# Transposes of the first unit in all PSUM buffers, evacuations split by buffer, and the second unit's transposes moved to the third and fourth store tile

## Chip, cores, metric

One core of a Trainium2 chip. The metric is the device time of one execution in microseconds.

## The reference

```python
def setup_inputs():
    batch, heads, seq, dim = 8, 8, 512, 64
    ...   # q and k, float32

def reference(q, k):
    scale = 1.0 / np.sqrt(q.shape[-1])
    return (np.einsum('bhqd,bhkd->bhqk', q, k) * scale).astype(np.float32)
```

q and k together are 16.78 MB, the scores 67.11 MB. Four bytes out for each byte in, and little arithmetic between.

## The kernel before

The batch is cut into four units. A unit's k and q are loaded into one "big" buffer (4.19 MB), cast to bf16 by GpSimd, transposed by TensorE into PSUM in eight groups of eight, and copied out of PSUM (VectorE and ScalarE take the groups in turn, four copies a group). A unit gives four store tiles of 4.19 MB. A store tile also takes a "big" buffer, is filled by eight evacuations of PSUM, and leaves in one DMA. Three "big" buffers serve loads and stores in turn.

```python
    big_pool = ctx.enter_context(tc.tile_pool(name="big", bufs=3))
    tpsum_pool = ...(name="tpsum", bufs=2, space=PSUM)      # transposes
    psum_pool = ...(name="psum", bufs=3, space=PSUM)        # scores

    def evacuate(dst, src):
        if n_evac % 6 in (0, 2, 3):
            pinned(nc.scalar.mul(out=dst, in_=src, mul=scale))
        else:
            pinned(nc.vector.tensor_scalar(out=dst, in0=src, scalar1=scale, ...))
        n_evac += 1

    # transpose(v, kb, qb) is a generator: 8 groups of 5 steps
    # (one step of 8 TensorE transposes, four steps of one PSUM copy)

    def scores(v, t):
        o = big_pool.tile([P, 2, RO, S], f32, name="big")
        for x in range(2):
            for i in range(0, RO, 2):
                ps = psum_pool.tile([P, 2, S], f32, name="ps")
                ...                                         # two matmuls
                evacuate(o[:, x, i:i + 2, :], ps)
                yield
        nc.sync.dma_start(out=out_r[v, t], in_=o...)

    cast = [load_and_cast(v) for v in range(UNITS)]
    for _ in transpose(0, *cast[0]):
        pass
    for v in range(UNITS):
        ahead = transpose(v + 1, *cast[v + 1]) if v + 1 < UNITS else iter(())
        for t in range(TILES):
            for n, _ in enumerate(scores(v, t)):
                take(ahead, 1 + (t > 0 if v == 0 else n % 4 == 3))
```

The order of work on each engine is the order of the program. So the last line is a schedule: it says beside which store tile the next unit's transposes are done.

## Time and profile before

| | before |
|---|---|
| median of the first 3 runs | 202.94 us (202.80 to 202.94) |
| span of the trace | 201.3 us |
| busiest compute engine | VectorE, 63% of the span |
| data queue, share of the 16 DMA engines' time | 98.1% |
| bytes at the steady 430 GB/s | 83.89 MB / 0.43 = 195.1 us |

In all lines of the profiler PE is TensorE's matmuls and PEld its weight loads, DVE is VectorE, ACT ScalarE, POOL GpSimd and SP the sync engine, which issues the DMAs; L82 is line 82 of the kernel.

### The profile page before, as it was taken

How to read it: one execution, taken by the hardware profiler on the slowest of the kernel's cores; microseconds unless marked ns; L12 is line 12 of the kernel's file. 1: busy time of each engine (PE TensorE's matmuls, PEld its weight loads, DVE VectorE, ACT ScalarE, POOL GpSimd, SP SyncE). 2: the span in 40 equal slices, each digit the busy share in tenths (PEclk: the TensorE clock that was granted, in tenths of full speed). 3: DMA queues.
4: the chain of work that ended last, by engine and by line, in shares of the span. 5: the costliest groups of instructions: out<-in, count | busy, mean ns of one | idle time of the engine just before them, and what ended most of it. 6: DMA issues, size and time to landing. Idle time of an engine off the chain costs nothing.

```text
span 201.3 us, 1456 instructions
## 1 busy us (share of the span) xinstructions
PE 99.2 (49%) x503; PEld 48.3 (24%) x512; DVE 126.4 (63%) x130; ACT 100.7 (50%) x129; POOL 30.6 (15%) x22
## 2 busy tenths in 40 slices
PE   0033366753976729463729554856535666710000
PEld 0033353321522414231315221432212222200000
DVE  6726659995989929796749796569635264530000
ACT  2016667786674856583837663856515341510000
POOL 1277777556000000000000000000000000000000
PEclk9999999998599996999975998888995857555555
DMA  6999999999999999999999999999999999999993
GB/s 205 430 443 430 420 433 440 420 407 427 433 436 425 422 443 427 430 423 440 430 423 433 433 430 427 440 430 423 433 436 430 410 446 433 420 423 433 433 427 163
DMA packets 5510, 83.97 MB, mean 417 GB/s; under 512 B 384, under 2 KB 384, under 8 KB 384
## 3 DMA queue, kind: packets, MB, share of 16 engines
q1 hardware_dynamic: 5504, 83.89, 98.1%
q8 instruction: 4, 0.07, 0.1%
q14 instruction: 2, 0.02, 0.0%
HBM read 16.78 MB, written 67.11 MB: 417 GB/s over the span
## 4 chain that ended last, share of the span: by engine, by line
DMA 63%; DVE 16%; PE 3%; POOL 3%; ACT 1%; POOLq 1%; issue 1%; SPq 0%; DVEq 0%; ACTq 0%
DMA out_dram<-big 43%; DMA big<-in_q_dram 20%; DVE big L66 12%; PE ps L132 3%; DVE qz L95 3%; POOL xb L82 3%; DVE kT L95 1%; ACT big L64 1%; POOLq L186 1%; SPq L78 0%; DVEq L66 0%; SPq L137 0%; ACTq L64 0%; POOLq L82 0%
## 5 line engine op out<-in xcount | busy, mean ns | idle before, releaser
L132 PE MATMUL ps<-kT,qz 128*128 128x512 bf16 x247 | 81.1, 450 | 55.1 <-ACT big L64 39.2
L66 DVE TENSOR_SCALAR big<-ps 128x1024 f32<-128x1024 f32 x64 | 76.3, 1222 | 39.9 <-DMA out_dram<-big 29.1
L64 ACT ACTIVATE big<-ps 128x1024 f32<-128x1024 f32 x64 | 63.7, 1023 | 57.0 <-DMA out_dram<-big 30.8
L132 PEld LDWEIGHTS <-qz 128*128 128x128 bf16 x256 | 27.5, 111 | 96.0 <-issue 83.2
L82 POOL CAST xb<-big 128x2048 bf16<-128x2048 f32 x16 | 29.9, 1896 | 17.6 <-DMA big<-in_k_dram 11.9
L95 DVE COPY kT<-tp 64x512 bf16<-64x512 bf16 x32 | 22.0, 687 | 6.3 <-PE tp L107 5.7
L95 ACT COPY kT<-tp 64x512 bf16<-64x512 bf16 x32 | 18.5, 578 | 14.7 <-PE tp L107 14.4
L95 DVE COPY qz<-tp 64x512 bf16<-64x512 bf16 x32 | 22.0, 687 | 3.1 <-PE tp L116 2.7
L95 ACT COPY qz<-tp 64x512 bf16<-64x512 bf16 x32 | 18.5, 578 | 3.9 <-PE tp L116 3.6
L107 PE MATMUL tp<-identity,xb 128*128 128x128 bf16 x128 | 12.0, 254 | 16.5 <-POOL xb L82 12.5
L116 PE MATMUL tp<-identity,xb 128*128 128x128 bf16 x128 | 12.8, 265 | 6.0 <-DVE kT L95 3.5
L107 PEld LDWEIGHTS <-xb 128*128 128x128 bf16 x128 | 10.5, 116 | 20.8 <-POOL xb L82 12.8
L116 PEld LDWEIGHTS <-xb 128*128 128x128 bf16 x128 | 11.3, 122 | 10.9 <-issue 8.9
L147 DVE MEMSET qz<- 128x4096 uint32 x2 | 6.9, 3472 | 2.5 <-PEq L175 1.7
L95 ACT ACT_TABLE_LOAD x1 | 1.3, 1283 | 0.7 <-PEq L175 0.7
masks.py:199 POOL TENSOR_SCALAR_AFFINE_SELECT identity<-identity 128x128 bf16<-128x128 bf16 x1 | 0.3, 294 | 0.1
masks.py:197 POOL MEMSET identity<- 128x128 bf16 x1 | 0.2, 205 | 0.3 <-POOLq L175 0.3
L175 POOL MEMSET const-float32-0.0<- 128x1 f32 x1 | 0.1, 99 | 0.2 <-issue 0.2
L175 POOL MEMSET const-bfloat16-1.0<- 128x1 bf16 x1 | 0.1, 102 | 0.0
L175 POOL MEMSET const-uint8-127<- 128x1 uint8 x1 | 0.1, 102 | 0.0
L175 POOL MEMSET const-float32-1.0<- 128x1 f32 x1 | 0.1, 99 | 0.0
## 6 DMA issues: line engine op xcount, KB each, us to landing
out_dram<-big SPq DMA_DIRECT2D x16, 4096.0 KB, 21.4
big<-in_k_dram SPq DMA_DIRECT2D x4, 2048.0 KB, 19.2
big<-in_q_dram SPq DMA_DIRECT2D x4, 2048.0 KB, 24.2
```

What stands on the lines that cost most here:

```text
L64: pinned(nc.scalar.mul(out=dst, in_=src, mul=scale))
L66: pinned(nc.vector.tensor_scalar(out=dst, in0=src, scalar1=scale, scalar2=None, op0=mybir.AluOpType.mult))
L82: pinned(nc.gpsimd.tensor_copy(out=xb[:, :, s, :], in_=xf[:, x, s].rearrange("p (j d) -> p j d", j=J)))
L95: pinned(copy(out=dst(s, h), in_=src[:, h]))
L107: pinned(nc.tensor.transpose(out=tp[:, j, :], identity=identity, in_=kb[:, j0 + j].rearrange("p s d -> p (s d)")))
L116: pinned(nc.tensor.transpose(out=tp[:, i, jj, :], identity=identity, in_=qb[:, RO * jj + i0 + i].rearrange("p s d -> p (s d)")))
L132: pinned(nc.tensor.matmul(out=ps[:, w, :], lhsT=qz[:, i + w, n, :], rhs=kT[:, n].rearrange("d m s j -> d (m s j)"), start=True, stop=True))
L147: nc.vector.memset(qz, 0.0)
L175: nc = _bacc.Bacc("TRN2", target_bir_lowering=False, num_devices=1)
L186: with _tile.TileContext(nc) as tc:
```

## The change

It means to get the first store out sooner. (1) Half of the first k cast moves from GpSimd to VectorE. (2) The first unit's transposes may also use the scores' PSUM buffers, which are idle then, so that groups need not wait for each other. (3) Evacuations go ScalarE, ScalarE, VectorE, so that with three buffers each buffer has one engine. (4) The second unit's transposes are not begun beside the first two store tiles, but done beside the third (three steps after each evacuation) and the fourth (two).

```diff
-        if n_evac % 6 in (0, 2, 3):
+        if n_evac % 3 < 2:
             pinned(nc.scalar.mul(out=dst, in_=src, mul=scale))
...
-                pinned(nc.gpsimd.tensor_copy(out=xb[:, :, s, :], ...
+                copy = nc.vector.tensor_copy if v == x == s == 0 else nc.gpsimd.tensor_copy
+                pinned(copy(out=xb[:, :, s, :], in_=...))
...
+        def transposed(rows):
+            if v == 0 and n_tp % 4 > 1:
+                tp = psum_pool.tile([P, W, P], bf16, name="ps")
+            else:
+                tp = tpsum_pool.tile([P, W, P], bf16, name="tp")
...
-                take(ahead, 1 + (t > 0 if v == 0 else n % 4 == 3))
+                take(ahead, (0, 0, 3, 2)[t] if v == 0 else 1 + (n % 4 == 3))
```

(The order in which the two PSUM pools are made also changes; the two transpose loops are folded into one helper.)

More of the change, by code (lines that the diff above doesn't have):

```diff
@@ L35 @@
     JJ = J // RO
-    IW = 8 // JJ
     TILES = N // 2
@@ L50 @@
     t_pool = ctx.enter_context(tc.tile_pool(name="t", bufs=2))
+    psum_pool = ctx.enter_context(tc.tile_pool(name="psum", bufs=3, space=bass.MemoryType.PSUM))
     tpsum_pool = ctx.enter_context(tc.tile_pool(name="tpsum", bufs=2, space=bass.MemoryType.PSUM))
-    psum_pool = ctx.enter_context(tc.tile_pool(name="psum", bufs=3, space=bass.MemoryType.PSUM))
     pinned = tc.keep_in_program_order
@@ L81, in load_and_cast @@
             for s in range(2):
-                pinned(nc.gpsimd.tensor_copy(out=xb[:, :, s, :],
-                                             in_=xf[:, x, s].rearrange("p (j d) -> p j d", j=J)))
+                copy = nc.vector.tensor_copy if v == x == s == 0 else nc.gpsimd.tensor_copy
+                pinned(copy(out=xb[:, :, s, :], in_=xf[:, x, s].rearrange("p (j d) -> p j d", j=J)))
             both.append(xb)
@@ L103, in transpose @@
         ts[v] = (kT, qz)
-        for j0 in range(0, J, 8):
-            tp = tpsum_pool.tile([P, 8, P], bf16, name="tp")
-            for j in range(8):
-                pinned(nc.tensor.transpose(out=tp[:, j, :], identity=identity,
-                                           in_=kb[:, j0 + j].rearrange("p s d -> p (s d)")))
+        W = 8
+        def transposed(rows):
[3 more added lines that the diff above has]
+                tp = tpsum_pool.tile([P, W, P], bf16, name="tp")
+            for w, row in enumerate(rows):
+                pinned(nc.tensor.transpose(out=tp[:, w, :], identity=identity,
+                                           in_=row.rearrange("p s d -> p (s d)")))
+            return tp
+        for j0 in range(0, J, W):
+            tp = transposed([kb[:, j0 + j] for j in range(W)])
             yield
             yield from rearrange(tp, "d j (n h m) -> d h n m j",
-                                 lambda s, h: kT[half(h), :, :, s, j0:j0 + 8])
+                                 lambda s, h: kT[half(h), :, :, s, j0:j0 + W])
+        IW = W // JJ
         for i0 in range(0, RO, IW):
-            tp = tpsum_pool.tile([P, IW, JJ, P], bf16, name="tp")
-            for i in range(IW):
-                for jj in range(JJ):
-                    pinned(nc.tensor.transpose(out=tp[:, i, jj, :], identity=identity,
-                                               in_=qb[:, RO * jj + i0 + i].rearrange("p s d -> p (s d)")))
+            tp = transposed([qb[:, RO * jj + i0 + i] for i in range(IW) for jj in range(JJ)])
             yield
-            yield from rearrange(tp, "d i jj (n h m) -> d h i n m jj",
+            yield from rearrange(tp.rearrange("p (i jj) c -> p i jj c", jj=JJ),
+                                 "d i jj (n h m) -> d h i n m jj",
                                  lambda s, h: qz[half(h), i0:i0 + IW, :, h * U:(h + 1) * U]
```

## The prediction

> **What bounds the kernel now.** I read the rates first, then the stores, then the chain, then the groups. The page first:
>
> ```profile
> span 201.3 us, 1456 instructions
> ...
> DMA  6999999999999999999999999999999999999993
> ...
> q1 hardware_dynamic: 5504, 83.89, 98.1%
> ...
> HBM read 16.78 MB, written 67.11 MB: 417 GB/s over the span
> ```
>
> No compute engine is above 63% (VectorE), but the 16 DMA engines are at nine tenths or more in 38 of 40 slices, and the data queue alone fills 98.1% of their time. So the first question is whether there is any stretch in which the DMA waits for the compute engines. I asked for busy time by stage, cut where loads (to 33 us), loads just before the first store (33 to 38), loads beside stores (38 to 45) and stores alone (from 45) begin, then for the last 18 us before the tail:
>
> ```profile
> 5.00:33.00 28.00, 11.18 (x89) 8.72 (x91) 17.04 (x21) 12.25 (x19) 18.67 (x10) 1.00 1.01 431
> 33.00:38.00 5.00, 2.69 (x22) 1.41 (x20) 4.89 (x6) 3.12 (x5) 3.74 (x2) 1.00 1.01 426
> 38.00:45.00 7.00, 4.51 (x31) 2.18 (x29) 6.84 (x9) 6.30 (x9) 3.74 (x2) 1.00 1.01 417
> 45.00:190.00 145.00, 80.85 (x369) 35.95 (x374) 94.31 (x97) 77.73 (x97) 3.74 (x2) 0.81 1.01 430
> ...
> 178.00:196.00 18.00, 0.00 (x0) 0.00 (x0) 0.15 (x1) 0.00 (x0) 0.00 (x0) 0.50 1.01 431
> ```
>
> The last two columns are DMA share and GB/s. The share is 1.01 in every stage: the DMA is never short of work. It moves 430 GB/s beside busy engines and 431 when all compute has ended. The one soft spot is 417 while loads and stores overlap, still fully busy. The arithmetic closes: 83.89 MB at 430 GB/s is 195.1 us; counting back from the 1.43 MB of data that I find moved by 6 us (332 GB/s from 2 to 6 us, 98 before, less 0.09 MB of instruction fetch), the stream starts in effect at 2.7 us, so it ends at 197.8. The trace has it thinning out from 197 to 198.5, then completion, and 201.3 is the end. The start (first load issue 0.74 us) and the tail (about 3 us) are touched by no line of the diff.
>
> The DMA can only be delayed if a store comes too late. Each store tile is 4.19 MB, 9.75 us at that rate. With the queue served about in order, all that is queued before store i runs out at 2.7 + (16.78 + 4.19 i)/0.43: 41.7, 51.5, 61.2, 71.0, 80.7 us for i = 0 to 4. When were the first four issued? From the timeline of the sync engine:
>
> ```profile
> 38.23 0.40 SPq L137 DMA_DIRECT2D out_dram<-big  x1
> 46.05 0.39 SPq L137 DMA_DIRECT2D out_dram<-big  x1
> 58.31 0.37 SPq L137 DMA_DIRECT2D out_dram<-big  x1
> 63.61 0.37 SPq L137 DMA_DIRECT2D out_dram<-big  x1
> ```
>
> Slack before the queue runs dry: 3.5, 5.4, 2.9 and 7.4 us; the fifth, at 71.19, has 9.5. It stays 8 to 10 us later (the last is issued at 178.21, against 188). The chain of waits shows why the third store is as late as 58.31:
>
> ```profile
> 17.70 27.22 DMA big<-in_q_dram
> ...
> 45.07 1.90 POOL xb L82
> 46.96 1.85 POOLq L186
> 48.81 0.02 issue
> 48.84 1.23 DVE big L66
> ```
>
> The three "big" buffers are shared by loads and store tiles. Tile 2 takes the buffer of the fourth unit's load, whose q lands at 44.92 and is cast by GpSimd until 48.81. By the same rotation tile 0 needs unit 1's casts done (27.1 us) and tile 1 unit 2's (36.9).
>
> The durations used below:
>
> ```profile
> L66 DVE TENSOR_SCALAR big<-ps 128x1024 f32<-128x1024 f32 x64 | 76.3, 1222 | 39.9 <-DMA out_dram<-big 29.1
> L64 ACT ACTIVATE big<-ps 128x1024 f32<-128x1024 f32 x64 | 63.7, 1023 | 57.0 <-DMA out_dram<-big 30.8
> L95 DVE COPY kT<-tp 64x512 bf16<-64x512 bf16 x32 | 22.0, 687 | 6.3 <-PE tp L107 5.7
> L95 ACT COPY kT<-tp 64x512 bf16<-64x512 bf16 x32 | 18.5, 578 | 14.7 <-PE tp L107 14.4
> ```
>
> The longest wait of both evacuating engines is for a store to land (29.1 and 30.8 us): they already wait for the DMA, not the DMA for them.
>
> [...]
>
> **The change, part by part.**
>
> First cast on VectorE. It starts when the memsets end (9.40 us; k has landed at 8.7) and beside it GpSimd does the other half (8.7 to 10.6). [...]PE began its transposes at 12.49. [...]The q casts wait for their load (13.57) and end at 17.3 either way, so unit 3's load is still issued at 17.33.
>
> First transposes in four PSUM buffers. Before, groups went in pairs: PE at 12.49, 16.83, 20.82, 25.12, and the last copy ended at 27.03 + 2.35 = 29.4. Now the k groups run without a stop: PE 11.8 to 15.6 (16 transposes took 1.89), VectorE from 12.8 does two groups of 4 x 0.69 (to 18.3), ScalarE two groups of 4 x 0.58. The q groups, ready at 17.3, follow in free buffers: VectorE 18.4 to 24.0. So unit 0 is ready at about 24 instead of 29.4: 5.4 us less. But tile 0's buffer is free only at 27.1, so 3.1 us of this is lost to a wait that takes its place.
>
> Tiles 0 and 1 without transposes. Evacuations now go ScalarE, ScalarE, VectorE: tile 0 has six on ScalarE, 6 x 1.02 = 6.1 us. Store 0 is issued at about 27.1 + 6.2 = 33.4 (before 38.2); store 1, from 36.9 with five (5.1 us), at about 42.4 (before 46.1).
>
> Tile 2 with 24 of the 40 transpose steps. It starts at 48.8 as before. VectorE has three evacuations (3.7) and eleven copies, of which two run before 48.8: 3.7 + 9 x 0.69 = 9.9 us; plus half a microsecond for PE where two transposes' buffers are handed over: 59.2, against 58.3. Its deadline is 61.2: slack 2.0. Tile 3 with 16 steps: ScalarE has six evacuations and six copies to its last one, 6.1 + 3.5 = 9.6, so 59 + 10 = 69; deadline 71.0, slack 2.0. Tile 4, at 5.4 ScalarE evacuations and four copies plus waits, some 8.2 us: 77.5 against 80.7. From there a tile takes about 8 us in a period of 9.75, and slack grows again.
>
> Whole-kernel load: ScalarE 86 x 1.02 + 64 x 0.58 = 125 us, VectorE 42 x 1.22 + 44 + 7 + 1 = 103: the two swap places, and neither is near 201.
>
> Sum on the path that sets the end: start 0, stream 0, tail 0. One small term: the stage of mixed loads and stores starts 4.8 us earlier, at 417 instead of 430 GB/s, which costs 4.8 x 0.03 = 0.15 us. 202.94 + 0.1 = 203.0.
>
> **The rivals.** (a) The earlier first store moves the end: the intent, and 4.8 us would make it 198. For it: the last store hangs from the first through three buffers. Against it: the DMA is full at 38 us and after; an earlier store only makes the queue longer. (b) A hole opens at 61 or 71 us. Transposes that ran in the idle time before 48.8 are now packed behind it, and slack falls to 2 us at two stores. Each microsecond beyond it is one on the end. If both tiles take 2 us more than I sum, tile 3 is 2 us late: 205. The 16 DMA engines also need not run dry together, so a small loss may begin before the deadline. This is my main risk. (c) ScalarE becomes the bound at two thirds of the evacuations: 5.45 + 2.3 = 7.8 us a tile, under 9.75; no. (d) Longer mixing of loads and stores delays unit 3's q (already 2 to 3 us behind the 4.9 us rhythm of the earlier loads): then tile 2 slips and (b) gets its time.
>
> **Range and chances.** Only (b) and (d) have size, and both lengthen; (a) is limited to what is not stream now, under 0.5 us. So the range is narrow below and wider above: 202.4 to 204.5. Faster by 2% would need 199: 1%. Slower by 2% needs a hole of 4 us: 4%.
>
> **What would show it.** The DMA row at nine in the same 38 slices and about 430 GB/s from 45 to 190 us; store 0 issued near 33 us and store 1 near 42, with the last store still landing at the same time; unit 0's last copy near 24 us, then a wait of some 3 us for GpSimd's cast; stores 2 and 3 near 59 and 69; ScalarE near 125 us and VectorE near 103. A slice under nine near 61 or 71 us would mean rival (b). An end earlier by more than a microsecond would prove me wrong about the stream.

What before's trace has is 430 GB/s beside work and 431 without, and 1896 ns for GpSimd's cast of 128x2048. The sum came to 202.94 + 0.1 = 203.0. From the 12.49 of before's trace the same steps end 0.7 us later, at 24.7, still ahead of the 27.1 at which tile 0's buffer is free, so the stores' times stand. The half microsecond for PE in tile 2 and the waits in tile 4's 8.2 us were estimates. That the 16 DMA engines need not run dry together is seen at the end of before's trace: their mean busy share is 0.69, 0.31 and 0.08 in the microseconds from 197, 198 and 199.

## The result

The changed kernel is correct and takes 203.31 us (median of 4; 203.16 to 203.41) against 202.94 of the kernel before (median of 4; 202.80 to 203.24). The ratio is 1.0015, with a 95% interval of 0.9998 to 1.0033: the same. Ratios here and below are the mean time of one kernel's fast runs over that of the other's of the same rounds, so not quite the ratio of the medians.

The page of the kernel after, its span, its DMA row, the data queue and the rate:

```profile
span 201.3 us, 1459 instructions
...
DMA  6999999999999999999999999999999999999993
...
q1 hardware_dynamic: 5504, 83.89, 98.1%
...
HBM read 16.78 MB, written 67.11 MB: 417 GB/s over the span
```

The DMA row is the same digit for digit. The stages of the kernel after, cut at the same times as in the prediction (start:end and length; busy us of PE, PEld, DVE, ACT and POOL, with instruction counts; granted clock, DMA share, GB/s):

```profile
5.00:33.00 28.00, 13.92 (x83) 8.96 (x85) 18.16 (x21) 14.83 (x22) 18.59 (x9) 0.88 1.01 431
33.00:38.00 5.00, 0.71 (x3) 0.19 (x2) 1.22 (x1) 1.48 (x3) 3.73 (x3) 0.96 1.00 423
38.00:45.00 7.00, 5.91 (x31) 2.78 (x32) 3.82 (x5) 3.65 (x4) 4.52 (x3) 0.78 1.01 410
45.00:190.00 145.00, 79.62 (x387) 36.58 (x393) 76.07 (x83) 99.72 (x123) 2.94 (x2) 0.82 1.01 430
```

The compute columns have changed in every row. The DMA share has not, and the last row's rate is 430 as before. Only the stage of loads beside stores is slower: 423 and 410 GB/s where it was 426 and 417.

The stores did move. The sync engine's timeline of the kernel after, first five stores (start, duration, engine, line, operation):

```profile
33.28 0.40 SPq L143 DMA_DIRECT2D out_dram<-big  x1
42.92 0.39 SPq L143 DMA_DIRECT2D out_dram<-big  x1
58.44 0.37 SPq L143 DMA_DIRECT2D out_dram<-big  x1
67.16 0.37 SPq L143 DMA_DIRECT2D out_dram<-big  x1
74.55 0.37 SPq L143 DMA_DIRECT2D out_dram<-big  x1
```

The first goes out 5.0 us sooner, the second 3.1 us sooner, the third at the same time, the fourth and fifth 3.6 and 3.4 us later. In the chain of waits of the kernel after, the third tile still hangs from the last load and its cast:

```profile
17.54 26.52 DMA big<-in_q_dram
...
44.21 1.89 POOL xb L82
46.10 1.85 POOLq L192
47.95 0.02 issue
47.98 1.22 DVE big L65
```

And the groups of the kernel after, the two evacuations and the two casts (busy us, mean ns of one, idle time before and what ended most of it):

```profile
L63 ACT ACTIVATE big<-ps 128x1024 f32<-128x1024 f32 x86 | 84.4, 1023 | 43.2 <-DMA out_dram<-big 20.0
L65 DVE TENSOR_SCALAR big<-ps 128x1024 f32<-128x1024 f32 x42 | 51.4, 1225 | 66.2 <-DMA out_dram<-big 34.3
L82 POOL CAST xb<-big 128x2048 bf16<-128x2048 f32 x15 | 29.8, 2012 | 16.9 <-DMA big<-in_k_dram 10.8
...
L82 DVE CAST xb<-big 128x2048 bf16<-128x2048 f32 x1 | 1.2, 1165 | 0.0
```

The page gives ScalarE 121.0 us busy (before 100.7) and VectorE 102.6 (126.4): they swapped places, and both evacuating groups still wait above all for stores to land.

### The profile page after: what moved, and what is told of

Its sections match the earlier page's. It is cut to its first block, busy times and chain, and to the rows that moved or that the text cites. A ratio compares the mean times of both kernels' runs of the same rounds, so it can differ in the third digit from the quotient of the medians.

```text
span 201.3 us, 1459 instructions
## 1 busy us (share of the span) xinstructions
PE 100.2 (50%) x503; PEld 48.5 (24%) x512; DVE 102.6 (51%) x109; ACT 121.0 (60%) x151; POOL 30.5 (15%) x21
## 3 DMA queue, kind: packets, MB, share of 16 engines
q1 hardware_dynamic: 5504, 83.89, 98.1%
## 4 chain that ended last, share of the span: by engine, by line
DMA 61%; ACT 9%; PE 7%; DVE 5%; POOL 3%; issue 1%; POOLq 1%; ACTq 1%; SPq 0%
DMA out_dram<-big 41%; DMA big<-in_q_dram 19%; ACT big L63 8%; PE ps L138 5%; POOL xb L82 3%; PE tp L111 2%; DVE big L65 2%; DVE kT L94 2%; DVE qz L94 1%; POOLq L192 1%; ACT kT L94 1%; ACT qz L94 1%; ACTq L192 0%; SPq L77 0%; ACTq L63 0%
## 5 line engine op out<-in xcount | busy, mean ns | idle before, releaser
L63 ACT ACTIVATE big<-ps 128x1024 f32<-128x1024 f32 x86 | 84.4, 1023 | 43.2 <-DMA out_dram<-big 20.0
L65 DVE TENSOR_SCALAR big<-ps 128x1024 f32<-128x1024 f32 x42 | 51.4, 1225 | 66.2 <-DMA out_dram<-big 34.3
L111 PE MATMUL tp<-identity,xb 128*128 128x128 bf16 x224 | 21.0, 252 | 18.1 <-POOL xb L82 13.6
L94 ACT COPY kT<-tp 64x512 bf16<-64x512 bf16 x28 | 16.2, 578 | 12.5 <-PE tp L111 12.2
L94 DVE COPY kT<-tp 64x512 bf16<-64x512 bf16 x28 | 19.2, 687 | 4.7 <-PE tp L111 4.4
L94 DVE COPY qz<-tp 64x512 bf16<-64x512 bf16 x28 | 19.2, 687 | 0.4
L94 ACT COPY qz<-tp 64x512 bf16<-64x512 bf16 x28 | 16.2, 578 | 0.5 <-PE tp L111 0.2
L111 PE MATMUL ps<-identity,xb 128*128 128x128 bf16 x32 | 3.8, 312 | 0.0
L94 DVE COPY kT<-ps 64x512 bf16<-64x512 bf16 x4 | 2.8, 689 | 0.1
L94 DVE COPY qz<-ps 64x512 bf16<-64x512 bf16 x4 | 2.8, 689 | 0.1
```

The source lines that it names most:

```text
L94: pinned(copy(out=dst(s, h), in_=src[:, h]))
L111: pinned(nc.tensor.transpose(out=tp[:, w, :], identity=identity, in_=row.rearrange("p s d -> p (s d)")))
```

## The experiments

All runs give the reference's result except where it is said. Times are medians. "Store 1" to "store 4" are the issue times of the first four stores in the trace. By the prediction's sum, all that is queued before them runs out at 41.7, 51.5, 61.2 and 71.0 us; I call these the dry times.

| run | store 1 | store 2 | store 3 | store 4 | us | ratio to before (95%) |
|---|---|---|---|---|---|---|
| before | 38.23 | 46.05 | 58.31 | 63.61 | 202.94 | |
| after | 33.28 | 42.92 | 58.44 | 67.16 | 203.31 | 1.0015 (0.9998 to 1.0033) |
| after_again | 33.41 | 43.05 | 59.26 | 67.97 | 203.28 | 1.0018 (1.0006 to 1.0031) |
| after_late2_x2 | 33.47 | 43.10 | 61.21 | 68.42 | 204.16 | 1.0070 (1.0048 to 1.0093) |
| after_late2_x6 | 33.55 | 43.47 | 66.94 | 74.68 | 209.77 | 1.0330 (1.0312 to 1.0348) |
| after_one_transpose | 33.49 | 43.12 | 54.92 | 60.58 | 202.39 | 0.9970 (0.9956 to 0.9983) |
| before_late0_x5 | 45.22 | 52.51 | 63.03 | 69.97 | 207.84 | 1.0236 (1.0218 to 1.0253) |
| after_late0_x5 | 39.83 | 45.30 | 58.33 | 67.05 | 203.29 | 1.0010 (0.9995 to 1.0025) |
| after_old_schedule | 34.95 | 46.69 | 57.13 | 64.35 | 203.33 | 1.0015 (1.0000 to 1.0030) |
| after_k_cast_dve | 33.47 | 42.75 | 59.63 | 68.35 | 203.44 | (one run) |
| before_late2_x2 | 38.10 | 45.93 | 61.09 | 66.26 | 202.99 | 1.0000 (0.9985 to 1.0016) |
| old_schedule_late2_x2 | 35.00 | 45.41 | 60.20 | 66.12 | 203.39 | 1.0020 (1.0005 to 1.0036) |
| before_evac_only | 37.63 | 46.61 | 57.59 | 64.84 | 203.23 | 1.0014 (1.0001 to 1.0028) |
| before_schedule_only | 35.22 | 44.02 | 60.46 | 71.92 | 205.00 | 1.0091 (1.0062 to 1.0120) |

### The changed kernel again

No edit, five rounds.

> The changed kernel once more, to see whether its 0.15% is real. Stream theory (the end is set by the bytes, and only the longer stretch of loads beside stores costs): ratio 1.0005 to 1.002, that is 0.1 to 0.4 us. Rival, the change opens a hole in the DMA now and then: ratios that scatter over 1.005 in some runs. Rival, pure noise: a ratio within 0.0005 of 1.

The ratio is 1.0018, and its interval now excludes 1: the change costs 0.1 to 0.6 us in this job. No run scatters upward (203.24 to 203.52), so the rival of an occasional hole falls.

### Less compute: one unit's transposes for all

```diff
-        ahead = transpose(v + 1, *cast[v + 1]) if v + 1 < UNITS else iter(())
+        ahead = iter(())
+        ts[v] = ts[0]
```

> Wrong result on purpose: units 1 to 3 use the first unit's transposes, so 96 PSUM copies on each of ScalarE and VectorE split (48 each, some 28 and 33 us) and 192 transposes fall away. Stream theory: 203.2 within 0.4. Chain rival: each tile's fill is shorter by 2 to 2.7 us, and the chain holds five or six fills: 10 to 15 us faster, 188 to 193.

The result is wrong. (The count in the expectation is put clumsily: 96 PSUM copies in all fall away, 48 on each engine.) The engines' busy time in the changed kernel, then in this one:

```profile
PE 100.2 (50%) x503; PEld 48.5 (24%) x512; DVE 102.6 (51%) x109; ACT 121.0 (60%) x151; POOL 30.5 (15%) x21
```

```profile
PE 100.5 (50%) x320; PEld 38.9 (19%) x320; DVE 70.5 (35%) x61; ACT 94.2 (47%) x103; POOL 30.5 (15%) x21
```

VectorE falls from 102.6 to 70.5 us busy and ScalarE from 121.0 to 94.2, and the time only to 202.39. That is 0.9 us less than after_again and 0.4 us below my band, and nowhere near the chain's 10 to 15 us. So the chain in which tiles wait for buffers does not bound the kernel; some 59 us of engine time are worth less than one microsecond. Why they are worth 0.9 us is not shown. The traces say where to look: the steady rate is hardly higher (431 against 430 GB/s from 45 to 190 us), but from 198 to 200 us after_again still moves 90 GB/s and this run 41, so less of its data is left for the end.

### A late third store, a little and a lot

```diff
                 evacuate(o[:, x, i:i + 2, :], ps)
+                if (v, t, x, i) == (0, 2, 1, RO - 2):
+                    for _ in range(2):              # 6 in the second run
+                        pinned(nc.vector.tensor_scalar(out=o[:, x, i:i + 2, :], in0=ps, ...))
```

> The changed kernel, with the last evacuation of the third store tile done twice more on VectorE (2 x 1.22 us), so that its store goes out at about 58.4 + 2.4 = 60.9 us. Stream theory, by which the queue runs dry at 61.2 us: 203.3, at most 0.3 more. Rival, the end hangs from the chain of tiles through the three buffers (each late tile hands its delay on): 203.3 + 2.4 = 205.7.

> The same with six repeats: the third store at about 58.4 + 7.3 = 65.8 us. Stream theory: the queue is dry from 61.2 to 65.8, a hole of 4.6 us, and the time is 203.3 + 4.6 = 207.9; the DMA row shows slices well below nine there. Chain rival: 203.3 + 7.3 = 210.6. Rival, the tile's slack is larger than the deadline formula says: under 206.

The long delay first. The DMA row of after_late2_x6 and its stages around the hole (same columns as above):

```profile
DMA  6999999999980999999999999999999999999995
```

```profile
60.00:61.00 1.00, 0.75 (x4) 0.23 (x3) 0.97 (x2) 0.67 (x2) 0.00 (x0) 1.00 1.07 459
61.00:62.00 1.00, 0.57 (x2) 0.19 (x2) 0.97 (x2) 0.99 (x3) 0.00 (x0) 1.00 0.26 107
62.00:66.94 4.94, 2.15 (x12) 1.20 (x11) 4.84 (x5) 3.64 (x5) 0.00 (x0) 0.63 0.02 7
66.94:67.50 0.56, 0.56 (x2) 0.16 (x2) 0.55 (x2) 0.00 (x0) 0.00 (x0) 0.50 0.00 0
67.50:68.00 0.50, 0.35 (x1) 0.00 (x0) 0.50 (x1) 0.00 (x0) 0.00 (x0) 0.50 1.23 524
68.00:69.00 1.00, 0.00 (x0) 0.00 (x0) 0.97 (x3) 0.00 (x0) 0.00 (x0) 0.50 0.61 262
```

These windows count a packet where it starts, with its whole length of some 0.6 us (98.1% of 16 x 201.3 us, over the page's 5504 packets less the 384 under 512 B). So a share above 1, or a rate of 524 GB/s, says that packets start together, not that they move faster; and the last packets run on for up to some 0.6 us after the queue is empty.

The DMA starts packets at the full rate until 61 us and for a quarter of the next microsecond: the queue runs dry at 61.3, where the sum had put 61.2. The store is issued at 66.94 (I had expected 65.8), and its first packets start 0.6 to 1.1 us after that: none from 66.94 to 67.50, 524 GB/s from 67.50 to 68.00. The loss is 209.77 - 203.28 = 6.5 us: 5.6 us from the dry time to the issue, and 0.9 us more, which I call the restart. The total is nearer to the chain rival's 210.6 than to the 207.9 that I forecast, because the store came 1.1 us later than in my sum and the restart was not in it. The trace decides between them: the DMA is idle only up to the start of that store. Without the repeats the store would have gone out at about 66.94 - 7.34 = 59.6 us. The first 1.7 us of delay, up to the dry time, were free (the chain would have charged them), and the restart took 0.9 us of that back.

The short delay shows the same edge from the other side. The store is issued at 61.21, at the dry time itself, and 0.9 us is lost. I had expected 0.3 at most. So here a store had to be issued some time before the queue ran dry; the runs below narrow down how long.

### A late first store, in both kernels

The same repeats on VectorE, five of them, in the first tile (`(0, 0, 1, RO - 2)`).

> The kernel before, with the last evacuation of the first store tile repeated five times on VectorE (6.1 us): first store at about 38.2 + 6.1 = 44.3 us. Stream theory with the deadline of 41.7 us: a hole of some 2.6 us (2 to 3.5, as the loads end raggedly), time 202.9 + 2.6 = 205.5. Rival, the first store has no bearing because loads still run: 203.

> The changed kernel with the same five repeats in the first store tile: first store at about 33.3 + 6.1 = 39.4 us, within its deadline of 41.7, and the second tile after it at 45 or 46, within 51.5. Stream theory: 203.3 within 0.4, so the change bought a margin that the kernel before lacks. Rival, the change made the start more delicate: over 204.5.

The DMA row of before_late0_x5, its first store, and its stages from 41 us to the issue:

```profile
DMA  6999999929999999999999999999999999999995
```

```profile
45.22 0.40 SPq L141 DMA_DIRECT2D out_dram<-big  x1
```

```profile
41.00:42.00 1.00, 0.27 (x5) 0.14 (x3) 0.96 (x2) 0.00 (x0) 0.77 (x1) 1.00 0.66 279
42.00:45.20 3.20, 0.00 (x1) 0.00 (x0) 3.13 (x4) 0.00 (x0) 0.98 (x1) 0.58 0.02 10
```

The ninth slice (41.2 to 46.4 us) is almost empty: the DMA starts packets for two thirds of the microsecond from 41, then almost none (shares of 0.66, 0.04, 0.04 and 0 in the microseconds from 41: the loads do end raggedly). The hole runs from the dry time of 41.7 to the issue at 45.22, 3.5 us (2.6 expected; the store slipped 7.0 instead of 6.1 us). The rest of the 4.65 us measured (207.84 - 203.19, the median of before in that job) is 1.1 us of restart. The changed kernel with the same delay takes 203.29: its first store, at 39.83, is in time. So here is what the change does buy: 5 us more room ahead of the first dry time, which this workload never uses.

### Each part by itself

```diff
 # after_old_schedule, from the changed kernel
-                take(ahead, (0, 0, 3, 2)[t] if v == 0 else 1 + (n % 4 == 3))
+                take(ahead, 1 + (t > 0 if v == 0 else n % 4 == 3))
 # before_evac_only, from the kernel before
-        if n_evac % 6 in (0, 2, 3):
+        if n_evac % 3 < 2:
 # before_schedule_only, from the kernel before
-                take(ahead, 1 + (t > 0 if v == 0 else n % 4 == 3))
+                take(ahead, (0, 0, 3, 2)[t] if v == 0 else 1 + (n % 4 == 3))
```

> The changed kernel with the old schedule of the second unit's transposes (beside tiles 1 to 4 of the first unit). Stream theory: 203.1 within 0.4; first store at 35 to 37 us, second at 44 to 46, third earlier than in the changed kernel (about 57). Rival, the schedule is what cost the 0.15%: the ratio to before drops under 1.0005.

> The kernel before with the new split of evacuations alone (two thirds on ScalarE). If the 0.15 to 0.18% of the changed kernel come from loads and stores overlapping longer: here the first store stays within 1 us of 38.2, and the ratio is 1.0000 to 1.0006. Rival, the split itself costs them: 1.0015 or more.

> The kernel before with the new schedule of the second unit's transposes alone. First store some 3 us earlier (about 35 us), third near 59. Overlap theory: half of the changed kernel's cost, ratio 1.0005 to 1.001. Rival, the schedule is the cost: 1.0015 or more. Rival, neither: 1.0000.

(The old schedule puts the 40 steps beside tiles 1 to 3, as 8 + 16 + 16, not 1 to 4.) Undoing the schedule in the changed kernel leaves the ratio at 1.0015, so there is no sign that the schedule costs the 0.2% there; the interval, 1.0000 to 1.0030, does not exclude it. The split of evacuations alone gives 1.0014 (1.0001 to 1.0028) with the first store at 37.63, hardly moved. That is close to the rival's figure, but the interval also holds my theory's 1.0000 to 1.0006. The stages of before_evac_only just before and during the overlap of loads and stores:

```profile
33.00:38.00 5.00, 3.69 (x28) 2.10 (x28) 4.17 (x6) 4.60 (x6) 3.65 (x2) 1.00 0.98 416
38.00:45.00 7.00, 4.67 (x32) 2.28 (x30) 6.51 (x9) 6.90 (x11) 3.73 (x2) 1.00 1.00 410
```

They are as slow as in the changed kernel (423 and 410 GB/s), though the first store went out only 0.6 us sooner than before. But one trace does not resolve this: after_old_schedule and old_schedule_late2_x2 run the same program up to 45 us and show 403 and 424 GB/s from 38 to 45. So what costs the 0.2% stays open, and parts (1) and (2) of the change were not run alone.

The schedule alone was the surprise: 0.9% slower, 203.66 to 205.53 us. The DMA row of before_schedule_only has a slice under nine, and its fourth store and stages show why:

```profile
DMA  6999999999999989999999999999999999999995
```

```profile
71.92 0.37 SPq L137 DMA_DIRECT2D out_dram<-big  x1
```

```profile
70.00:71.00 1.00, 0.39 (x8) 0.39 (x7) 0.97 (x2) 0.98 (x2) 0.00 (x0) 1.00 1.05 442
71.00:72.00 1.00, 0.73 (x7) 0.34 (x5) 1.00 (x2) 0.92 (x2) 0.00 (x0) 1.00 0.37 156
72.00:73.00 1.00, 0.94 (x4) 0.30 (x4) 0.85 (x2) 0.71 (x1) 0.00 (x0) 1.00 0.62 262
```

This is rival (b) of the prediction, come true in a kernel with a part of the change: with the transposes packed beside the third and fourth tile and the old split, the fourth store is issued at 71.92, after the dry time of 71.0, and the queue runs empty in the microsecond from 71. Of its delay against the changed kernel (4.8 us), 2.0 us come from the third store (60.46 against 58.44) and 2.7 from the fourth tile itself. The stages between the third and the fourth store, of before_schedule_only and then of the changed kernel:

```profile
60.40:72.00 11.60, 7.28 (x48) 3.61 (x46) 10.36 (x13) 9.51 (x14) 0.00 (x0) 0.92 0.95 404
```

```profile
58.40:67.20 8.80, 5.63 (x42) 2.98 (x41) 8.61 (x11) 8.60 (x13) 0.00 (x0) 1.00 1.02 435
```

In the first, VectorE has 10.36 us of work in 11.6 us. In the second the two engines have 8.61 and 8.60 us in 8.8: the work is even, and the tile takes 2.7 us less. (The old split gives the fourth tile four evacuations on VectorE, the new one two.) So the new schedule with the old split runs late, and the changed kernel, which has the new split beside the other parts, does not.

### The same small delay in two more kernels

Two repeats in the third tile, as in after_late2_x2.

> The kernel before with two repeats (2.44 us) in its third store tile: third store at about 58.3 + 2.4 = 60.8 us. From the runs so far, time is lost from some 0.9 us before the queue runs dry at 61.3: loss about 0.4 us, 203.3 to 203.7. Rival, the kernel before has more room here than the changed one: no loss, 203.0.

> The changed kernel with the old schedule and the same two repeats: third store at about 57.1 + 2.4 = 59.6 us, before 60.4 (61.3 less 0.9). No loss beyond the 0.3 us that the old schedule showed without repeats: ratio 1.001 to 1.0025, and below that of the changed kernel with the same repeats (1.007). Rival, the repeats cost the same wherever they stand: 1.007.

The changed kernel with the old schedule issues its third store at 60.20 and loses nothing (203.39; 203.33 without the repeats). The kernel before stands on the edge: its median, 202.99, is the rival's "no loss" and not the loss of 0.4 us that I forecast. But in its profiled run the store goes out at 61.09 and the run takes 204.06; its four other runs take 202.89 to 203.06. Their traces were not kept, so that their stores were a few tenths earlier is likely, but not shown.

### Both halves of the first k cast on VectorE

```diff
-                copy = nc.vector.tensor_copy if v == x == s == 0 else nc.gpsimd.tensor_copy
+                copy = nc.vector.tensor_copy if v == x == 0 else nc.gpsimd.tensor_copy
```

> The changed kernel with both halves of the first k cast on VectorE. If the single VectorE cast delayed GpSimd's half (3.67 us instead of 1.89) because the two shared something, then with GpSimd out of it two casts of 1.17 us end at 9.3 + 2.3 = 11.7, and the transposes start there instead of 12.3. Rival, the cast on VectorE waits for something else: no change from 12.3. Time 203 in both.

The timeline of the kernel before, then of the changed kernel, then of this one (start, duration):

```profile
8.71 3.73 POOL L82 CAST xb<-big 128x2048 bf16<-128x2048 f32 x2 [7.41 <-DMA big<-in_k_dram]
12.49 1.63 PEld L107 LDWEIGHTS <-xb 128*128 128x128 bf16 x16 [12.49 <-POOL xb L82]
```

```profile
8.56 3.67 POOL L82 CAST xb<-big 128x2048 bf16<-128x2048 f32 x1 [7.26 <-DMA big<-in_k_dram]
9.32 1.17 DVE L82 CAST xb<-big 128x2048 bf16<-128x2048 f32 x1
12.28 3.33 PEld L111 LDWEIGHTS <-xb 128*128 128x128 bf16 x32 [12.28 <-POOL xb L82]
```

```profile
9.32 2.29 DVE L82 CAST xb<-big 128x2048 bf16<-128x2048 f32 x2
11.67 3.29 PEld L111 LDWEIGHTS <-xb 128*128 128x128 bf16 x32 [11.67 <-DVE xb L82]
```

One cast by GpSimd beside one by VectorE (3.67 us, "x1") takes as long as two casts by GpSimd alone (3.73, "x2"), so giving half away gained 0.2 us. How much of even that is the load is not shown: GpSimd's cast begins at 8.71 us in before and at 8.56 in the changed kernel. In three traces with the pair of casts (after, after_again, after_old_schedule) GpSimd's is recorded from 8.56, 8.67 and 8.56 us and ends at 12.22 or 12.23, some 1.75 us after VectorE's end at 10.48 or 10.49; VectorE's takes 1.16 or 1.17 us, as in the run without GpSimd beside it (two in 2.29). Why the delay falls on GpSimd's is not shown. With GpSimd out of it the transposes start at 11.67, as expected. The time stays at 203 (203.44, a single run).

## Why the prediction was right

**The bound.** Right, and shown: a full DMA row, one rate, 59 us of compute removed for under 1 us of time, and holes where a store comes at its dry time, just before it or after it, and nowhere else in the kept traces. The forecast of 203.0 (202.4 to 204.5) met 203.31. That no higher rate is to be had was not shown: the traces have 430 GB/s for stores alone and 431 for loads alone, with a DMA share of 1.01 in both. And one reading was loose: the stream does not end at 198.5; before's trace still moves 33 GB/s between 199 and 200 us.

**The dry times.** Right to a tenth or two: the queue emptied at 61.3 (61.2 predicted) and two thirds into the microsecond after 41 (41.7). What the step left out is the restart. A store issued at the dry time is already late: 0.9 to 1.1 us is lost on top of the hole. So the third store's room in the changed kernel is smaller than its distance to 61.2. Third stores at 60.20 and 60.46 (old_schedule_late2_x2 and before_schedule_only) still met a full queue (DMA shares of 1.04 and 0.97 from 61 to 62 us), those at 61.09 and 61.21 (before_late2_x2 and after_late2_x2) did not (0.49 and 0.33). So a store had to come between 0.2 and 0.8 us before 61.3; against 60.46, the changed kernel's 58.44 and 59.26 leave 1.2 to 2.0 us.

**Stores.** Predicted 33.4, 42.4, 59.2, 69 and 77.5; measured 33.28, 42.92, 58.44, 67.16 and 74.55. The first three are right. (The third tile began at 47.98 instead of 48.8, as the last load landed sooner in this trace; it took 10.5 us, where I had summed 10.4. In after_again it began at 48.79 and its store went out at 59.26.) For the fourth I charged ten microseconds after the third; it took 8.7, with both evacuating engines 98% busy. ScalarE began the fourth tile's evacuations at 57.79, while VectorE was still at the third's last one (until 58.4), and I had set one after the other. The fifth inherits 1.8 us of this, and it took 7.4 us itself, where I had summed some 8.2. Two sums of the prediction don't close: 36.9 + 5.1 is 42.0 and not 42.4 for the second store, and 69 + 8.2 is 77.2 and not 77.5 for the fifth.

**Unit 0.** Ready at 24 predicted, from a start at 11.8; the last copy ended at 24.6, from a start at 12.28. The wait that takes the gain's place is there: 2.4 us (VectorE) and 3.1 us (ScalarE) until 26.98, for GpSimd's cast.

**First cast.** Wrong in size: the gain measured is 0.2 us, less than the one predicted. The delay fell on GpSimd's half (3.67 us instead of 1.9), where I had charged it to VectorE's. It had no bearing on the end.

**The small term.** The overlap stage lost (430 - 426) x 5/430 + (430 - 417) x 7/430 = 0.26 us before and (430 - 423) x 5/430 + (430 - 410) x 7/430 = 0.41 after: 0.15 us, as predicted, but by luck. The prediction had the rate of the overlap unchanged and its stage longer; of the 0.15 us, 0.11 come from a lower rate between 38 and 45 us, where both kernels overlap loads and stores. Nor is it shown to be the cause of the 0.3 us measured, or even to be real: the same sum for before_evac_only gives 0.49, and for the two runs with the old schedule, alike up to there, 0.57 and 0.26. (In all traces whose first store was out by 38.3 us the rate from 38 to 45 is 400 to 424 GB/s.) The 0.3 us are at the edge of what the rounds resolve (before itself ran from 202.78 to 203.44).

**The rivals.** (b), called the main risk, was real: one part of the change alone runs into it. (a) fell: the first store went out 5.0 us sooner and the end stayed. So did (c): ScalarE is busy for 60% of the span. (d) did not come: unit 3's q landed at 44.06 us, and at 44.92 before.

## What to carry to other kernels

Where the DMA queue is full from end to end, ask of a change only two things: does it alter the bytes or their rate, and does any store come after the queue would run dry. The dry times are one division each (start + bytes queued before / rate), they held to a tenth or two here, and a store needed up to 0.8 us of room besides. Here an earlier first store (by 5.0 us) bought room, not time (ratio 1.0015); and work that was put off to later tiles used up their room (before_schedule_only: the fourth store at 71.92 against 71.0, ratio 1.0091), so look at the latest store, not the first.
